# Four moves in the order of work of a one-core decoder layer: compression weights split a turn ahead, a norm behind the values' second blob, late query heads between attention blocks, two output blobs in the projection's buffers

## The chip, the cores and the metric

The kernel runs on one core of a Trainium2 chip. The core has a matrix engine (TensorE, PE in the profile; its weight loads are PEld), a vector engine (VectorE, DVE), a scalar engine (ScalarE, ACT), GpSimd (POOL) and SyncE (SP), whose queue issues most of the loads here. Each engine runs its own instructions in a fixed order and waits on semaphores for the others. The metric is the device time of one execution in microseconds, as the median of several runs; smaller is better. One further execution was taken by the hardware profiler, and every row below is from that one.

## What is computed

The reference is one layer of a hybrid decoder on 512 tokens of width 2048, all in float32:

```python
mod = silu(c) @ w_ada + b_ada            # shift1, scale1, gate1, shift2, scale2, gate2
h   = rms_norm(x, norm1_g) * (1 + scale1) + shift1
u   = h @ w_in      # conv B, C, H | queries | K and V of three branches | gates
y_conv = B * causal_depthwise_conv3(C * H)
k_cmp, v_cmp = compress(K), compress(V)  # gelu(flat @ w1) @ w2 over blocks of 32 tokens
y_attn = compressed, selected and sliding-window attention, summed with sigmoid gates
x   = x + gate1 * ([rms_norm(y_conv) | rms_norm(y_attn)] @ w_out)
h   = rms_norm(x, norm2_g) * (1 + scale2) + shift2
x   = x + gate2 * (relu(h @ w_ff1)**2 @ w_ff2)
out = rms_norm(x, normf_g)
```

There are 8 query heads of 128 in two groups (2 key and value heads), so attention runs as 2 groups times 4 blocks of 128 queries.

## The kernel before

**Splitting.** Every float32 operand of a matmul is split into a high part `hi`, written by ScalarE as float32r, and a low part `lo = x - hi`, written by VectorE. `mm3` (lines 93 to 95) then adds three products: high times high (L93), high times low (L94), low times high (L95). A weight blob of 128 x 1024 thus costs one load of 512 KB (L73 or L781, SyncE's queue), one ScalarE copy (L83 or L789) and one VectorE subtraction (L84 or L790), and feeds 24 matmuls of 512 columns.

**Buffers.** Three pools matter. `mainp` has 29 slots of one tile each for everything that lives long (hidden states `h_m`, `part`, `kwin`, `cs`, conv outputs `y`, queries `q`, the conditioning weights `wa`, and the compression's `chi`, `clo`, `swh`, `swl`). `stage` has three raw buffers `raw`, two `wh` and two `wl`, through which all projection blobs go; a compression blob uses `raw` too but is split into two `mainp` slots (`spare=True`). `ffp` holds the buffers of the later stages (`rw`: six raw ones, `hl`: three split pairs). It is opened when `stage` and the attention's pools are closed and lies where they lay: in the program of before, the three `hl` buffers lie over `attc` and `raw`, the first `rw` buffer over the last `raw` buffer and the first `wh`, the second over both `wh`, the third over the second `wh`, the fourth over the second `wh` and the first `wl`, the fifth over both `wl`, the sixth over the second `wl`. An `ffp` buffer waits for the last reader of each old buffer under it (`reuse_waits="tile"`).

**Order.** Up to line 406 all instructions keep the written order (`pin`). From there on a scheduler orders each engine when the program is built: of the instructions that it estimates to be ready, the one written first goes first. The order on the chip is then fixed; SyncE's queue too is served in order.

**The stages around the change.** (1) The eight conv channels (L510 to 539) call `project` 16 times; each call runs two halves, each with one blob and 24 matmuls. After each half, `tick()` takes one step of the background list, first `compress(0)`, then `compress(1)`, and `more_ada(1)` loads two conditioning blobs and reduces them on VectorE (L134). A compression has two steps that build its operands (`ct`, `chi`, `clo`, L445 to 462), eight steps with one blob each (L464 to 472: load, split, 12 matmuls of 256 columns), and a tail. (2) `row_norm` of the conv output (L543) sums `sacc` over channels with four one-column matmuls (L171), takes a square root on ScalarE (L178, with a table load), a reciprocal, spreads it with a 128 x 512 matmul (L189, L192) and copies it to `rc` (L182), which `mixed` (L581) reads. (3) The values, gates and remaining keys: per group four blobs of 1072 columns, each with 48 matmuls of 268 columns (L548 to 569). (4) The queries; raw heads go to `raws`. `head(n)` (L573) turns one with five VectorE and one ScalarE instruction (`rope_split`). Heads 0 to 3 are made in the background, heads 4 to 7 at L734, ahead of attention. (5) Attention (L743 to 747): per block the scores go through three PSUM buffers `s`; one or two `out_conv` (24 matmuls each, the conv half of the output product) are written behind each block and fill the matrix engine's waits. (6) The attention half's norm, `mixa`, the last two `out_conv` (L753 to 763), then the product with `w_oa` (L812 to 817): eight blobs through `rw` and `hl`, and after each an `ada` with two more `rw` loads. The feed-forward stages follow.

Of the kernel before, what the change touches and what calls it, by code (L numbers as in the profile page):

```python
# [21 lines left out]
NR = 4  # L22
# [18 lines left out]
def hybrid_layer(ctx: ExitStack, tc: tile.TileContext, a, out):  # L41
# [34 lines left out]
    def weights(src, cols=1024, spare=False):  # L76
        raw = load(src, cols)
        if spare:
            wh, wl = slot(F32R, name="swh"), slot(F32R, name="swl")
        else:  # L80
            wh = stage.tile([P, BLOB], F32R, name="wh")
            wl = stage.tile([P, BLOB], F32R, name="wl")
        pin(nc.scalar.activation(wh[:, :cols], raw[:, :cols], AF.Copy))  # L83
        pin(nc.vector.tensor_tensor(out=wl[:, :cols], in0=raw[:, :cols], in1=wh[:, :cols].bitcast(F32),  # L84
                                    op=OP.subtract))
        return wh, wl
# [5 lines left out]
    def mm3(ps, lh, ll, rh, rl, start, stop, more=False):  # L92
        pin(nc.tensor.matmul(ps, lh, rh, start=start, stop=False, skip_group_check=more))  # L93
        pin(nc.tensor.matmul(ps, lh, rl, start=False, stop=False, skip_group_check=more))  # L94
        pin(nc.tensor.matmul(ps, ll, rh, start=False, stop=stop, skip_group_check=more))  # L95
# [72 lines left out]
    def row_norm(bank, square, width, dst, t0=0, t1=NQ):  # L168
        total = bank()
        for t in range(t0, t1):  # L170
            nc.tensor.matmul(total[:, t:t + 1], square[:, t * P:(t + 1) * P], ones[:, 0:1],  # L171
                             start=True, stop=True)
        row_bcast(bank, total[:, t0:t1], width, dst[:, t0 * P:t1 * P])
# [177 lines left out]
    w = (wh0, wl0)  # L351
# [89 lines left out]
    def compress(which, src):  # L441
        pe = cw2[:, which * 32:which * 32 + 32]
        w2 = [cw2[:, 64 + (which * 2 + i) * P:64 + (which * 2 + i + 1) * P] for i in range(2)]
        parts = []
        for hf in range(2):  # L445
            t = slot(name="ct")
            nc.vector.memset(t[:, 1024:SLOT], 0.0)
            tv = t[:, :1024].rearrange("p (l g n) -> p l g n", g=NG, n=32)
            n = 32 - hf
            for g in range(NG):  # L450
                nc.vector.tensor_tensor(
                    out=tv[:, :, g, :n],
                    in0=src[g].rearrange("p (n l) -> p l n", l=16)[:, :, hf:],
                    in1=pe[:, hf * 16:hf * 16 + 16, None].to_broadcast([P, 16, n]), op=OP.add)
            if hf:
                nc.vector.memset(tv[:, :, :, 31:], 0.0)
            hi = slot(F32R, name="chi")
            lo = slot(F32R, name="clo")
            nc.scalar.activation(hi, t, AF.Copy)
            nc.vector.tensor_tensor(out=lo, in0=t, in1=hi.bitcast(F32), op=OP.subtract)  # L460
            parts.append((hi, lo))
            yield
        pc = bank()
        for blk in range(8):  # L464
            wh, wl = weights(a["cmp_w1"][which * 8 + blk], spare=True)
            hi, lo = parts[blk // 4]
            for j in range(4):
                l = blk * 4 + j
                s = slice(j * 256, (j + 1) * 256)
                m = slice((l % 16) * 64, (l % 16) * 64 + 66)  # L470
                mm3(pc[:66, :256], hi[:, m], lo[:, m], wh[:, s], wl[:, s], l == 0, l == 31)
            yield
        hid = temp([P, 256], name="hid")[:64]
        tt = temp([P, 256], name="htt")[:64]
        nc.scalar.activation(hid, pc[:64, :256], AF.Copy)
        nc.vector.tensor_tensor(out=tt, in0=hid, in1=hid, op=OP.mult)
        nc.vector.tensor_scalar(tt, tt, 0.044715, 1.0, op0=OP.mult, op1=OP.add)
        nc.vector.tensor_tensor(out=tt, in0=tt, in1=hid, op=OP.mult)
        nc.scalar.activation(tt, tt, AF.Tanh, scale=math.sqrt(2.0 / math.pi))
        nc.vector.tensor_scalar(tt, tt, 1.0, 0.5, op0=OP.add, op1=OP.mult)  # L480
        nc.vector.tensor_tensor(out=hid, in0=hid, in1=tt, op=OP.mult)
        pt = bank()
        for i in range(2):
            nc.tensor.transpose(pt[:, i * 64:i * 64 + 64], hid[:, i * P:(i + 1) * P], ident[:64, :64])
        hidt = temp([P, 2, NG, 32], name="hidt")
        nc.scalar.activation(hidt.rearrange("p i g n -> p (i g n)"), pt[:, :P], AF.Copy)
        yield
        if which == 0:
            pk = bank()
            for i in range(2):  # L490
                nc.tensor.matmul(pk[:, :64], w2[i], hidt[:, i].rearrange("p g n -> p (g n)"),
                                 start=i == 0, stop=i == 1)
            for g in range(NG):
                split(kslc[g][:, :, :32], pk[:, g * 32:g * 32 + 32])
        else:
            pad = temp([P, 2, NG, P], name="hpad")
            nc.vector.memset(pad, 0.0)
            nc.vector.tensor_copy(pad[:, :, :, :32], hidt)
            for g in range(NG):
                pv = bank()  # L500
                for i in range(2):
                    nc.tensor.matmul(pv[:, :P], pad[:, i, g], w2[i], start=i == 0, stop=i == 1)
                split(vcmp[:, g], pv[:, :P])
# [36 lines left out]
    while background:  # L540
        tick()
    rc = accum("rc")
    row_norm(bank, sacc, 1024, rc)  # L543


    gates = attc.tile([P, NQ, NG, NR, 3], F32, name="gates")
# [1 line left out]
    for g in range(NG):  # L548
        pv = [bank() for _ in range(NQ)]
        for blk in range(4):  # L550
            wh, wl = weights(a["w_v"][g * 4 + blk], BLOB)
            more_ada(1)
            for j in range(4):
                k = blk * 4 + j
                s = slice(j * 268, (j + 1) * 268)
                for t in range(NQ):
                    c = slice(t * P, (t + 1) * P)
                    mm3(pv[t][:, :268], hs[k][:, 0, c], hs[k][:, 1, c], wh[:, s], wl[:, s],
                        k == 0, k == NK - 1)
        for t in range(NQ):  # L560
            if t % 2 == 0:
                vp = pair(F32R, name="vv").rearrange("p h (t c) -> p h t c", t=2)
            vv[g, t] = vp[:, :, t % 2]
            nc.scalar.activation(vv[g, t][:, 0], pv[t][:, :256], AF.Copy)
            nc.vector.tensor_tensor(out=vv[g, t][:, 1], in0=pv[t][:, :256],
                                    in1=vv[g, t][:, 0].bitcast(F32), op=OP.subtract)
            gt = gates[:, t, g].rearrange("p r b -> p (r b)")
            nc.scalar.activation(gt, pv[t][:, 256:268], AF.Tanh, scale=0.5)
            nc.vector.tensor_scalar(gt, gt, 1.0, 0.5, op0=OP.add, op1=OP.mult)
# [3 lines left out]
    def head(n):  # L573
        q = pair(F32R, name="q")
        for _ in rope_split(q, raws[n], SCALE):
            pass
        qs.append(q)
# [153 lines left out]

    for m in range(2):
        out_conv(m)
    for n in range(NR, 2 * NR):  # L734
        head(n)
    ya = []
    m = 2
    for g in range(NG):
        for r in range(NR):
            if r % 2 == 0:  # L740
                y2 = pair(name="ya")
            ya.append(y2[:, r % 2])
        for qb in range(NQ):  # L743
            attention(g, qb)
            for _ in range(1 + g):
                out_conv(m)
                m += 1
# [6 lines left out]
    for j in range(8):  # L754
        y = ya[j]
        nc.vector.scalar_tensor_tensor(out=y, in0=y, scalar=vec[:, V_GA + j:V_GA + j + 1], in1=ra,
                                       op0=OP.mult, op1=OP.mult)
        mt = pair(F32R, name="mixa")
        split(mt, y)
        mixa.append(mt)  # L760
        if j % 4 == 0:
            out_conv(m)
            m += 1
    att.close()
    front.close()

# [17 lines left out]
    def hl_tile():  # L784
        t = ffp.tile([P, 2, 1024], F32R, name="hl", bufs=3)
        return t[:, 0], t[:, 1]

    def hilo(dst, src):
        nc.scalar.activation(dst[0], src, AF.Copy)  # L789
        nc.vector.tensor_tensor(out=dst[1], in0=src, in1=dst[0].bitcast(F32), op=OP.subtract)  # L790
        return dst
# [18 lines left out]
    sacc = accum()  # L810
    pm = [bankf() for _ in range(8)]
    for k in range(8):  # L812
        wh, wl = hilo(hl_tile(), raw_blob(a["w_oa"][k]))
        for i in range(8):
            s = slice(i * P, (i + 1) * P)
            mm3(pm[i], wh[:, s], wl[:, s], mixa[k][:, 0], mixa[k][:, 1], k == 0, k == 7)
        ada(M_G2 * NK + 8 + k, raw_blob)
# [406 lines left out]
```

## Time and profile before

| what | value |
|---|---|
| median of 3 runs | 2229.99 us (2229.52 to 2233.65) |
| the profiled execution, whole | 2229.29 us |
| its span, first to last instruction | 2227.5 us |
| mean granted TensorE clock | 0.979 |
| transferred | 453.62 MB, 204 GB/s mean |

The profile's page gives busy time per engine, a chain of waits, and groups of instructions. Windows are stretches of the span with busy time of each engine (number of instructions in brackets), the clock granted to TensorE (1 is full speed) and DMA. A timeline row gives start and duration in us, engine, line, what is written and read, and in square brackets how long the engine had been idle before it and what ended that. A row of waits gives total us, number of times and the longest.

### The profile page before, as it was taken

To read this page: it belongs to the slowest core of one execution; us is meant where nothing else is said; L and a number is where in the kernel's file an instruction comes from. 1 tells how busy PE (TensorE), PEld (TensorE's weight loads), DVE (VectorE), ACT (ScalarE), POOL (GpSimd) and SP (SyncE) were. 2 spreads that over 40 slices of the span, in tenths; PEclk is the share of its full clock that TensorE was granted. 3 is DMA by queue.
4 is the path that set the end of the run, shared out by engine and by line. 5 is a ranking of instruction groups with operands and counts; after the bars stand their busy time and mean duration, and the time that the engine had idled before them with its cause. 6 is when DMAs were issued, how large, how long until landed. Compare 5 with 4: busy or idle time off the path is not lost.

```text
span 2227.5 us, 37650 instructions
## 1 busy us (share of the span) xinstructions
PE 2134.3 (96%) x14942; PEld 1974.1 (89%) x14942; DVE 1918.9 (86%) x2998; ACT 1009.3 (45%) x1468; POOL 193.6 (9%) x366
## 2 busy tenths in 40 slices
PE   6999899999999989799999999999899999999996
PEld 4777778798787769799999999999899999999996
DVE  8889988777586677999999999999899999999996
ACT  4431333322354434665666556666333333333353
POOL 0000000000000001021111111113211011001000
PEclk8999999999999999899999999999999999999998
DMA  8985677855211165276666666668865466366432
GB/s 343 338 324 179 254 291 284 342 187 192 86 39 57 57 251 189 83 240 200 203 189 197 206 206 201 196 193 277 309 232 210 150 229 237 127 222 244 164 122 95
DMA packets 143984, 453.62 MB, mean 204 GB/s; under 512 B 15808, under 2 KB 20160, under 8 KB 143808
## 3 DMA queue, kind: packets, MB, share of 16 engines
q1 hardware_dynamic: 92192, 323.27, 40.8%
q0 software_dynamic: 51616, 127.95, 17.2%
q8 instruction: 117, 1.92, 0.3%
q14 instruction: 59, 0.48, 0.1%
HBM read 383.00 MB, written 68.16 MB: 203 GB/s over the span
## 4 chain that ended last, share of the span: by engine, by line
PE 77%; DVE 6%; ACT 2%; issue 1%; DMA 1%; POOL 0%; DVEq 0%; ACTq 0%; POOLq 0%
PE pf L95 19%; PE pf L93 19%; PE pf L94 19%; PE ps L95 4%; PE ps L94 4%; PE ps L93 4%; PE pw L95 1%; PE pw L93 1%; PE pw L94 1%; DVE hl L790 1%; PE pt L709 1%; PE pv L93 1%; PE pv L94 1%; ACT hl L789 0%; PE pv L95 0%
## 5 line engine op out<-in xcount | busy, mean ns | idle before, releaser
L95 PE MATMUL pf<-tk,hl 128*128 128x256 f32 x3576 | 1006.0, 282 | 12.7 <-DVE hl L790 12.7
L93 PE MATMUL pf<-tk,hl 128*128 128x256 f32 x3576 | 1008.3, 282 | 9.9 <-ACT hl L789 9.2
L94 PE MATMUL pf<-tk,hl 128*128 128x256 f32 x3576 | 1006.4, 282 | 1.2 <-DVE tk L861 1.2
L95 PEld LDWEIGHTS pf<-tk,hl 128*128 128x128 f32 x3576 | 677.4, 190 | 15.2 <-DVE hl L790 15.2
L93 PEld LDWEIGHTS pf<-tk,hl 128*128 128x128 f32 x3576 | 678.6, 190 | 12.5 <-ACT hl L789 11.8
L94 PEld LDWEIGHTS pf<-tk,hl 128*128 128x128 f32 x3576 | 677.8, 190 | 1.6 <-DVE tk L861 1.5
L789 ACT ACTIVATE hl<-rw 128x1024 fp32r<-128x1024 f32 x266 | 281.0, 1057 | 300.6 <-PE pf L95 267.4
L790 DVE TENSOR_TENSOR hl<-rw,hl 128x1024 fp32r<-128x1024 f32 x266 | 324.0, 1218 | 32.2 <-ACT hl L789 31.7
L789 ACT ACTIVATE hl<-sg 128x1024 fp32r<-128x1024 f32 x189 | 200.3, 1061 | 264.0 <-PE pf L95 243.7
L790 DVE TENSOR_TENSOR hl<-sg,hl 128x1024 fp32r<-128x1024 f32 x189 | 230.3, 1219 | 41.9 <-ACT hl L789 40.9
L134 DVE SCALAR_TENSOR_TENSOR scr<-wa,cs 128x1024 bf16<-128x1024 f32 x176 | 210.1, 1218 | 3.3 <-DMA wa<-in_w_ada 3.2
L83 ACT ACTIVATE wh<-raw 128x1024 fp32r<-128x1024 f32 (+1 forms) x103 | 108.8, 1060 | 219.4 <-PE ps L94 106.2
L84 DVE TENSOR_TENSOR wl<-raw,wh 128x1024 fp32r<-128x1024 f32 (+1 forms) x103 | 126.2, 1226 | 54.1 <-ACT wh L83 53.5
L864 DVE TENSOR_TENSOR sg<-sg,rw 128x1024 f32<-128x1024 f32 x126 | 153.4, 1218 | 0.9
L95 PE MATMUL ps<-h_m,wl 128*128 128x512 f32 x360 | 142.7, 396 | 2.4 <-DVE wl L84 2.4
L93 PE MATMUL ps<-h_m,wh 128*128 128x512 f32 x360 | 142.7, 396 | 1.5 <-DVE part L384 1.0
L94 PE MATMUL ps<-h_m,wh 128*128 128x512 f32 x360 | 141.7, 394 | 0.0
L1038 DVE SCALAR_TENSOR_TENSOR x<-pf,mod,x 128x256 f32<-128x256 f32 x256 | 119.9, 478 | 14.2 <-PE pf L95 11.9
L93 PE MATMUL ps<-h,wh 128*128 128x512 f32 x280 | 113.4, 405 | 7.2 <-ACT wh L83 3.3
L95 PE MATMUL ps<-h,wl 128*128 128x512 f32 x280 | 114.0, 407 | 3.9 <-DVE wl L84 3.9
L94 PE MATMUL ps<-h,wh 128*128 128x512 f32 x280 | 113.2, 404 | 0.0
L1004 POOL DMA_DIRECT2D g<-gt x192 | 101.0, 532 | 86.9 <-DVE gt L861 81.5
(308 smaller groups left out, 2981.6 us busy)
## 6 DMA issues: line engine op xcount, KB each, us to landing
rw<-in_w_f SPq DMA_DIRECT2D x262, 512.0 KB, 4.4
wa<-in_w_ada SPq DMA_DIRECT2D x176, 512.0 KB, 6.0
tk<-g POOLq DMA_DIRECT2D x114, 512.0 KB, 8.6
g<-gt POOLq DMA_DIRECT2D x192, 256.0 KB, 4.9
raw<-in_w_conv SPq DMA_DIRECT2D x32, 512.0 KB, 6.7
g<-gb POOLq DMA_DIRECT2D x36, 256.0 KB, 2.3
raw<-in_w_kv SPq DMA_DIRECT2D x16, 512.0 KB, 5.4
raw<-in_w_cv SPq DMA_DIRECT2D x16, 512.0 KB, 4.1
```

The costliest lines, as they stand in the source:

```text
L83: pin(nc.scalar.activation(wh[:, :cols], raw[:, :cols], AF.Copy))
L84: pin(nc.vector.tensor_tensor(out=wl[:, :cols], in0=raw[:, :cols], in1=wh[:, :cols].bitcast(F32), op=OP.subtract))
L93: pin(nc.tensor.matmul(ps, lh, rh, start=start, stop=False, skip_group_check=more))
L94: pin(nc.tensor.matmul(ps, lh, rl, start=False, stop=False, skip_group_check=more))
L95: pin(nc.tensor.matmul(ps, ll, rh, start=False, stop=stop, skip_group_check=more))
L134: pin(nc.vector.scalar_tensor_tensor(out=scr, in0=w, scalar=1.0, in1=cs[i].rearrange("p a b -> p (a b)"), op0=OP.mult, op1=OP.mult, accum_ ...
L709: nc.tensor.transpose(pt[:, r * P:(r + 1) * P], probs[b, r][:, kb * P:(kb + 1) * P], ident)
L789: nc.scalar.activation(dst[0], src, AF.Copy)
L790: nc.vector.tensor_tensor(out=dst[1], in0=src, in1=dst[0].bitcast(F32), op=OP.subtract)
L864: nc.vector.tensor_tensor(out=dst, in0=x, in1=y, op=op)
L1004: nc.gpsimd.dma_start(out=gd[p // 4][idx[j]][p % 4 // 2][:, p % 2], in_=g[:, j])
L1038: nc.vector.scalar_tensor_tensor(out=xm, in0=src, scalar=gate, in1=xm, op0=OP.mult, op1=OP.add)
```

## The change

`compress` takes the weights of blob 0 at the end of its second operand step and those of each later blob behind the matmuls of the one before, where it took them ahead of its own matmuls. The norm's call moves from in front of the values into their first group, behind the second blob's matmuls. Heads 4 to 7 are no longer made in a row ahead of attention, but one behind each block of the first group, ahead of that block's `out_conv`. The first two `w_oa` blobs are taken by `weights` (buffers `raw`, `wh`, `wl`) at the end of attention, before the pools are closed, and the loop over `w_oa` uses them for k = 0 and 1.

```diff
@@ compress
             parts.append((hi, lo))
+            if hf:
+                w = weights(a["cmp_w1"][which * 8], spare=True)
             yield
         pc = bank()
         for blk in range(8):
-            wh, wl = weights(a["cmp_w1"][which * 8 + blk], spare=True)
+            wh, wl = w
             hi, lo = parts[blk // 4]
...
                 mm3(pc[:66, :256], hi[:, m], lo[:, m], wh[:, s], wl[:, s], l == 0, l == 31)
+            if blk < 7:
+                w = weights(a["cmp_w1"][which * 8 + blk + 1], spare=True)
             yield
@@ conv norm and values
     rc = accum("rc")
-    row_norm(bank, sacc, 1024, rc)
...
                         k == 0, k == NK - 1)
+            if g == 0 and blk == 1:
+                row_norm(bank, sacc, 1024, rc)
@@ attention
         out_conv(m)
-    for n in range(NR, 2 * NR):
-        head(n)
...
             attention(g, qb)
+            if g == 0:
+                head(NR + qb)
             for _ in range(1 + g):
@@ output product
             m += 1
+    oa = [weights(a["w_oa"][k]) for k in range(2)]
     att.close()
     front.close()
...
     for k in range(8):
-        wh, wl = hilo(hl_tile(), raw_blob(a["w_oa"][k]))
+        wh, wl = oa[k] if k < 2 else hilo(hl_tile(), raw_blob(a["w_oa"][k]))
```

## The prediction

> **What bounds the kernel now.** I read the page's busy times first, then who waited for whom on the matrix engine, then windows of 20 us, and last the timelines of the four places that the change touches.
>
> ```profile
> span 2227.5 us, 37650 instructions
> PE 2134.3 (96%) x14942; PEld 1974.1 (89%) x14942; DVE 1918.9 (86%) x2998; ACT 1009.3 (45%) x1468; POOL 193.6 (9%) x366
> ```
>
> The matrix engine is busy 96% of the span; time can be won only where it stands still, or runs at a low clock after standing still. It idles 93 us in all. The windows show how much of that lies where the change works:
>
> ```profile
> 260.00:280.00 20.00, 14.48 (x74) 11.72 (x72) 19.92 (x34) 8.01 (x9) 0.00 (x0) 0.96 0.74 277
> 280.00:300.00 20.00, 17.81 (x75) 14.51 (x76) 16.32 (x26) 7.18 (x8) 0.00 (x0) 0.78 0.76 277
> 340.00:360.00 20.00, 20.00 (x94) 16.48 (x93) 19.13 (x32) 6.39 (x7) 0.00 (x0) 1.00 0.87 322
> 600.00:620.00 20.00, 17.47 (x88) 14.73 (x87) 18.63 (x57) 9.47 (x31) 0.00 (x0) 0.83 0.13 43
> 680.00:700.00 20.00, 18.55 (x88) 14.69 (x88) 11.27 (x37) 8.14 (x27) 0.00 (x0) 0.91 0.02 6
> 780.00:800.00 20.00, 14.83 (x62) 10.86 (x60) 15.94 (x25) 9.57 (x17) 0.00 (x0) 0.93 0.11 39
> ```
>
> Columns: window, length, then busy time (instructions) of PE, PEld, DVE, ACT, POOL, then granted clock, DMA share, GB/s. Lost are 5.5 + 2.2 us around the first compression, 2.5 in the first attention block, 5.2 ahead of `w_oa`, and in each the clock falls under 1. The second compression (340 to 360) loses nothing.
>
> **Part A, the compression.** The waits of 260 to 300, engine by engine:
>
> ```profile
> 274.64 0.34 PE L94 MATMUL ps<-swl,chi 128*66 128x256 f32 x1 [1.67 <-DVE swl L84]
> 280.37 0.48 PE L93 MATMUL ps<-swh,chi 128*66 128x256 f32 x1 [4.22 <-ACT swh L83]
> 282.67 0.80 PE L95 MATMUL ps<-h,wl 128*128 128x512 f32 x1 [1.82 <-DVE wl L84]
> 273.62 0.42 SPq L73 DMA_DIRECT2D raw<-in_cmp_w  x1
> 279.26 1.06 ACT L83 ACTIVATE swh<-raw 128x1024 fp32r<-128x1024 f32 x1 [0.81 <-DMA raw<-in_cmp_w]
> 281.39 1.22 DVE L84 TENSOR_TENSOR wl<-raw,wh 128x1024 fp32r<-128x1024 f32 x1
> ```
>
> Three waits, 7.7 us. The longest is for the third blob's load, issued only at 273.62, when a raw buffer came free. With each split written a turn earlier, its raw buffer is free a turn earlier and that load with it: I take the 4.2 us as gone. The other two are VectorE's, which is busy 19.92 of 20 us. No VectorE work is removed; one split more (1.22 us, the row at 281.39) now stands ahead of each conv blob's subtraction. So A = -4.2 + 1.2 = **-3.0**. The ends: all three waits gone and with them the slow stretch behind (14 matmuls of 512 columns between 282.67 and 288.79, 0.43 us apart where they need 0.23: 2.9 us), -10.6; nothing gained and the split more paid, +1.2. The number of loads and instructions is unchanged; two slots of `mainp` are held a turn longer (a rival below).
>
> **Part B, the conv norm.**
>
> ```profile
> 440.15 0.40 PE L95 MATMUL ps<-h_m,wl 128*128 128x512 f32 x1
> 443.46 1.05 PE L171 MATMUL ps<-ones,sacc 128*128 128x1 f32 x8 [2.91 <-DVE sacc L539]
> 445.90 2.04 PE L192 MATMUL ps<-dg,ones 128*128 128x512 f32 x2 [1.38 <-DVE dg L189]
> 446.95 1.21 PE L93 MATMUL ps<-wh,h 128*128 128x268 f32 x1
> 449.08 0.34 PE L93 MATMUL ps<-wh,h 128*128 128x268 f32 x1
> 449.39 0.28 PE L95 MATMUL ps<-wh,h 128*128 128x268 f32 x1
> 441.53 1.28 DVE L84 TENSOR_TENSOR wl<-raw,wh 128x1072 fp32r<-128x1072 f32 x1 [0.25 <-ACT wh L83]
> 786.42 1.10 PE L192 MATMUL pt<-dg,ones 128*128 128x512 f32 x2
> ```
>
> From the last conv matmul's end (440.15 + 0.23) to the first value matmul pass 6.57 us. The norm's own matmuls need 1.05 + 1.10 = 2.15 of that (the second as it ran at full clock at 786.42). Up to 449.08 the values' first seven matmuls take 2.13 us where at 0.123 us each (449.39 and after) they need 0.86: 1.27 more. The second value blob was split by 442.8, so the first was before; nothing else stops the values from starting at 440.4. B = -(6.57 - 2.15) - 1.27 = **-5.7**. Behind the second blob, at about 440.4 + 2 x 5.9 = 452.2 (48 matmuls of 0.123 each), `sacc` (443.4) is long done. The chain from L171 to L192 waits through a table load, the root, a reciprocal and L189:
>
> ```profile
> 783.75 1.28 ACT L178 ACT_TABLE_LOAD   x1
> 785.05 0.30 ACT L178 ACTIVATE rs<-tot,eps 128x4 f32<-128x4 f32 x1
> 785.38 0.18 DVE L179 RECIPROCAL rs<-rs 128x4 f32<-128x4 f32 x1 [0.38 <-ACT rs L178]
> 785.59 0.69 DVE L189 TENSOR_TENSOR dg<-vec,rs 128x512 f32<-128x512 f32 x1
> ```
>
> 2.5 us, covered by the third blob's matmuls; uncovered, B shrinks to -3.2, its other end. `rc` then comes near 457.6 instead of 448.6; its readers (`mixed`) feed the conv half of the output product, over 100 us later. No load is moved.
>
> **Part C, the late heads.**
>
> ```profile
> L281 DVE SCALAR_TENSOR_TENSOR q<-rs,q x8: 679/688/694, 544.5 to 608.6; 128x512 fp32r<-128x512 f32 x8
> 602.55 0.19 DVE L673 TENSOR_TENSOR pc<-s,cst 128x32 f32<-128x32 f32 x1
> 602.89 0.47 PE L663 MATMUL s<-kslc,q 128*128 128x160 f32 x1 [2.41 <-DVE pc L673]
> ```
>
> A head is five VectorE instructions of about 0.69 us; four heads are 13.7 us (20 x 0.69), and they end at 608.6, inside the first attention block. There a score buffer comes free only with L673, which stands behind them, and the matrix engine waits 2.41 us. Written behind the block, the heads fill VectorE's pauses instead. They don't vanish: each instruction can hold a short reduction of blocks 0 to 3 by up to 0.69 us. The second group's first block (680 to 700) has no heads and still idles 1.45 us at clock 0.91. I take 600 to 620 to become like it: (2.53 - 1.45) + 20 x (0.91 - 0.83) = 1.1 + 1.6 = **-2.7**. Ends: the idle 2.5 and all of the clock's 20 x 0.17 = 3.4 us, -5.9; only moved about, 0.
>
> **Part D, the first two output blobs.**
>
> ```profile
> 795.84 0.74 DVE L640 SCALAR_TENSOR_TENSOR x<-pw,mod,raw 128x512 f32<-128x512 f32 x1
> 796.61 0.33 SPq L781 DMA_DIRECT2D rw<-in_w_oa  x1
> 796.99 0.90 SPq L781 DMA_DIRECT2D rw<-in_w_ada  x2
> 797.93 0.43 SPq L781 DMA_DIRECT2D rw<-in_w_oa  x1
> 798.60 1.38 DVE L90 TENSOR_TENSOR mixa<-ya,mixa 128x512 fp32r<-128x512 f32 x2
> 801.71 0.80 PE L93 MATMUL pf<-mixa,hl 128*128 128x512 f32 x1 [6.55 <-ACT hl L789]
> 804.85 1.06 ACT L789 ACTIVATE hl<-rw 128x1024 fp32r<-128x1024 f32 x1 [3.19 <-DMA rw<-in_w_oa]
> 815.63 0.40 PE L95 MATMUL pf<-mixa,hl 128*128 128x512 f32 x1
> SPq L781 <- DVE x L640: 24.9, 1, 24.9
> ```
>
> Now the first `rw` load waits for the last `out_conv`'s residual, because it lies over a `raw` buffer; the matrix engine stands 6.55 us, and k = 1 ends at 815.9. After: k = 0 has its high part early and starts at 795.5. VectorE is full with `mixa` to 800.0, so the low part ends at 801.2 (1.22 us); 16 high-part matmuls (0.23 each) can go first, to 799.2, then 2.0 us of waiting; 32 matmuls later, at 808.6, k = 1 ends. That is 7.3 us ahead.
>
> What is late next is k = 2. All six `rw` buffers lie over the `wh` and `wl` that k = 0 and 1 now use until then. SyncE's queue has, in written order, two `ada` loads for k = 0, two for k = 1, then k = 2's blob. The first may go when k = 0 is done; the second lies over both `wh` and waits for k = 1's last L94, at 808.3, and three loads wait behind it. In the burst of before, the fourth load, issued as the second `rw<-in_w_oa` row, landed 804.85 - 796.61 = 8.2 us after the first issue. So k = 2's blob lands at 816.5, is copied by 817.6, and k = 2 starts 1.7 us later than now, waits 0.4 more for its low part (1.22 us, of which two slow matmuls of 0.43 cover the most) and, after 9 us of rest, runs 12 matmuls at the slow spacing (12 x 0.20 = 2.4). D = 1.7 + 0.4 + 2.4 = **+4.5**, a loss. Ends: written order kept inside k = 0, so that only two matmuls go ahead of the low part (3.2 more rest, and slow after it, 2.4), +10.1; no blocking at all, -7.3. I take the blocking, since the row of 24.9 us shows that these buffers do wait for what lies under them.
>
> Whether the 2.0 us rest inside k = 0 slows the clock is open: after 1.67 us (274.64) the next matmuls ran at full spacing, after 2.41 (602.89) they didn't. I take the nearer row, no. [...] By the trace's stricter reading the sum would be 2.4 us higher.
>
> **Sum.** -3.0 - 5.7 - 2.7 + 4.5 = -6.9 on the profiled execution's own 2229.3 us (span 2227.5 and 1.8 around it): 2222.4. That execution lies 0.7 under the median of the runs, so the forecast is 2223.
>
> **Rivals.**
>
> *D isn't blocked.* If the loads for k = 2 can start at 796.6 as now, D is -7.3 and the time 2229.3 - 3.0 - 5.7 - 2.7 - 7.3 = 2210.6. For it: the trace shows only the first `rw` load waiting, not the others. Against it: the order of SyncE's queue and the buffers' places.
>
> *VectorE only moves its work.* A = +1.2 and C = 0, with B and D as forecast: 2229.3 + 1.2 - 5.7 + 4.5 = 2229.3, no change. For it: 19.92 of 20 us in 260 to 280.
>
> *Slots run out: slower.* Two split blobs at once hold four of 29 `mainp` slots, so `wa` loads wait for compression matmuls, and the conv blob's load queues behind them:
>
> ```profile
> SPq L147 <- PE ps L95: 10.8, 8, 3.9
>   ACT wh L83: 35.7, 11
> ```
>
> The first row is SyncE's queue waiting for slots that compression matmuls release, 1.35 us each; the second, from who waits for the conv blobs' loads, shows that ScalarE already waits 11 times for one. At one such wait more per blob, all reaching the matrix engine, 16 x 1.35 = 21.6 us come on top in place of A's gain: 2229.3 + 21.6 - 5.7 - 2.7 + 4.5 = 2247.0. It decides from the turn on in which a conv blob is split later than the one before it is used up. Against it: 340 to 360 is full at 20.00 with the same loads, and the scheduler sends a load that is ready ahead of one that waits for a slot.
>
> **Chances.** Forecast 0.50, D unblocked 0.20, work only moved 0.17, slots 0.13. What a measurement of this kernel tells from no change is about 0.2%, 4.5 us (its runs spread over 4.1). Within the forecast, where A and D have wide ends, I give 0.72 to faster, 0.24 to same, 0.04 to slower; moved work is same at 0.75 and slower at 0.2; the outer two count whole. That makes 0.57 faster, 0.25 same, 0.18 slower. The forecast's own ends, taken as not all at once, are 2213 to 2232. The range reaches below to the unblocked case and above past the moved work, but not to the slots: 2207 to 2236.
>
> **What would show it.** A: the matrix engine's 4.2 us wait for `swh` is gone and 300 to 440 stays full. B: values start right behind the last conv matmul, and L192 waits under 0.5 us. C: 600 to 620 reads like 680 to 700. D: `w_oa` starts near 795.5 on the old scale, the second `rw` load comes only when k = 1 is done, and a wait of about 9 us for ScalarE's `hl` stands ahead of k = 2. I am wrong if that wait is missing, or if new waits appear at conv blobs between 300 and 440.

## The result, and the profile after

The changed kernel takes 2225.53 us (median of 10 runs, 2221.58 to 2228.79), the kernel before beside it 2231.85 (10 runs): the ratio is 0.9978, 95% interval 0.9970 to 0.9986, so 3.1 to 6.7 us faster. The forecast was 2223. The total came out; three of its four terms did not.

The page's head and the windows of 20 us of the changed kernel (columns as before):

```profile
span 2222.4 us, 37638 instructions
PE 2133.1 (96%) x14942; PEld 1971.6 (89%) x14942; DVE 1918.5 (86%) x2998; ACT 1008.6 (45%) x1468; POOL 193.6 (9%) x366
```

```profile
260.00:280.00 20.00, 13.85 (x75) 10.97 (x73) 18.41 (x30) 7.43 (x8) 0.00 (x0) 0.92 0.66 235
280.00:300.00 20.00, 17.73 (x72) 14.02 (x73) 17.07 (x26) 8.85 (x9) 0.00 (x0) 0.82 0.78 291
440.00:460.00 20.00, 20.00 (x161) 19.52 (x159) 15.35 (x27) 6.24 (x8) 0.00 (x0) 1.00 0.37 130
580.00:600.00 20.00, 17.62 (x84) 15.21 (x83) 9.85 (x32) 6.72 (x21) 0.00 (x0) 0.86 0.29 105
600.00:620.00 20.00, 19.63 (x103) 15.23 (x102) 15.37 (x40) 9.47 (x28) 0.00 (x0) 0.97 0.00 1
780.00:800.00 20.00, 18.61 (x78) 14.34 (x77) 16.60 (x26) 7.33 (x11) 0.00 (x0) 1.00 0.39 134
800.00:820.00 20.00, 17.05 (x66) 13.07 (x65) 17.54 (x29) 5.12 (x5) 0.00 (x0) 0.91 1.01 399
```

Read them against the old ones. The first compression (260 to 300) is no fuller: 31.58 us busy of 40, before 32.29. The values' window (440 to 460) is full. The first attention block's loss has moved along with the block, which starts 6.2 us earlier and so now lies in 580 to 600 (17.62 at clock 0.86; before 17.47 at 0.83). `w_oa` starts early, at 788.96, and 2.95 us of rest are left in 800 to 820.

Windows shift against each other, so the stages are better compared by the time between two matmuls that both kernels have. All entries are differences of start times in the traces (us):

| stage, from one matmul to the next named | before | changed | A only (e1) | B only (e2) | C only (e3) | D only (e4) | e9 | e10 | e11 |
|---|---|---|---|---|---|---|---|---|---|
| conv and compression: last projection to last conv matmul | 216.24 | 217.17 | 217.94 | 214.62 | 215.02 | 215.03 | 211.19 | 205.08 | 215.31 |
| norm and values: to the last value matmul | 55.43 | 50.22 | 56.44 | 50.19 | 56.43 | 56.32 | 50.19 | 50.23 | 50.19 |
| queries, attention: to the last `out_conv` matmul | 299.19 | 299.10 | 299.84 | 299.43 | 298.86 | 299.85 | 298.97 | 298.60 | 298.82 |
| `w_oa`: to its last matmul | 54.33 | 51.08 | 52.34 | 54.28 | 52.68 | 51.02 | 51.48 | 53.39 | 51.43 |
| to the 201st feed-forward matmul that has `tk` | 94.03 | 97.27 | 95.68 | 94.04 | 95.87 | 96.41 | 95.47 | 97.44 | 96.62 |

(e9 to e11 come below.) The two profiled executions differ by 5.1 us. Of that, 1.7 us was there before the first changed instruction: the last projection matmul starts at 223.92 and at 222.24. The stages between give +0.9, -5.2, -0.1, -3.2 and +3.2, and what follows gives +1.0. The columns also show how far one execution scatters where nothing was changed: the first row reads 214.62 to 216.24 without part A, the fourth 52.34 to 54.33 without part D.

**A: the same six loads, another blob behind them.** SyncE's queue in the kernel before, a row that the prediction does not show, and the next one:

```profile
263.64 9.93 SPq L147 DMA_DIRECT2D wa<-in_w_ada  x6
273.62 0.42 SPq L73 DMA_DIRECT2D raw<-in_cmp_w  x1
269.94 1.22 DVE L84 TENSOR_TENSOR swl<-raw,swh 128x1024 fp32r<-128x1024 f32 x1
```

The third row is VectorE's last read of the raw buffer that this load takes (by the addresses of the built program, the first compression blob's). The buffer was free at 271.16, and the load went 2.5 us later.

The same queue in the changed kernel, and the matrix engine's waits of half a microsecond or more there:

```profile
263.84 9.96 SPq L147 DMA_DIRECT2D wa<-in_w_ada  x6
273.86 0.42 SPq L73 DMA_DIRECT2D raw<-in_w_conv  x1
274.33 0.42 SPq L73 DMA_DIRECT2D raw<-in_cmp_w  x1
```

```profile
268.61 0.33 PE L93 MATMUL ps<-swh,chi 128*66 128x256 f32 x1 [0.54 <-ACT swh L83]
274.76 0.33 PE L94 MATMUL ps<-swl,chi 128*66 128x256 f32 x1 [1.55 <-DVE swl L84]
282.00 0.80 PE L93 MATMUL ps<-h,wh 128*128 128x512 f32 x1 [5.73 <-ACT wh L83]
```

In both kernels six conditioning loads occupy SyncE's queue for ten microseconds, since three of them (four in the changed kernel) wait for `mainp` slots. Before, the third compression blob stood behind them; now that blob is ahead of them and a conv blob stands behind. The 4.2 us wait for `swh` is gone and a 5.7 us wait for `wh` has come.

**B** went as forecast. The values' first matmul follows the last conv matmul directly, at 439.64; the norm's matmuls come 12 us later and wait for nothing:

```profile
439.41 0.39 PE L95 MATMUL ps<-h_m,wl 128*128 128x512 f32 x1
439.64 0.29 PE L93 MATMUL ps<-wh,h 128*128 128x268 f32 x1
451.48 0.95 PE L171 MATMUL ps<-ones,sacc 128*128 128x1 f32 x8
452.84 1.28 ACT L178 ACT_TABLE_LOAD   x1
455.96 1.02 PE L192 MATMUL ps<-dg,ones 128*128 128x512 f32 x2
```

**C.** The first attention block, now without a head in it (VectorE and the matrix engine):

```profile
591.89 1.23 DVE L84 TENSOR_TENSOR wl<-raw,wh 128x1024 fp32r<-128x1024 f32 x1 [0.97 <-ACT wh L83]
593.03 0.48 DVE L672 TENSOR_REDUCE nm<-s 128x1 f32<-128x128 f32 x2
593.84 0.19 DVE L678 TENSOR_TENSOR pc<-s,cst 128x32 f32<-128x32 f32 x1 [0.33 <-ACT p L675]
594.09 0.34 PE L668 MATMUL s<-kslc,q 128*128 128x160 f32 x1 [2.38 <-DVE pc L678]
```

The wait for `pc` is 2.38 us; it was 2.41. VectorE has pauses all round, but in its fixed order the subtraction of an `out_conv` blob stands first and the scores' maximum behind it; VectorE idles 0.97 us for that subtraction's `wh`, while the first scores' four matmuls had started at 589.97 to 590.27. In the kernel before, two instructions of a head stood right ahead of the instruction that ended the wait (602.55):

```profile
601.13 0.69 DVE L269 TENSOR_TENSOR rt<-qr,rot 64x512 f32<-64x512 f32 x1
601.84 0.69 DVE L271 TENSOR_TENSOR rt<-qr,rot 64x512 f32<-64x512 f32 x1
```

So other work stands in the place of the heads, and the wait is as long.

**D.** SyncE's queue and the two subtractions that release it, then `w_oa`'s first matmul, the rest inside k = 0, and the 49th matmul:

```profile
779.33 17.45 SPq L787 DMA_DIRECT2D rw<-in_w_ada  x4
796.83 0.42 SPq L787 DMA_DIRECT2D rw<-in_w_oa  x1
```

```profile
793.65 0.33 SPq L787 DMA_DIRECT2D rw<-in_w_ada  x1
795.98 0.80 SPq L787 DMA_DIRECT2D rw<-in_w_ada  x2
```

```profile
792.36 1.22 DVE L84 TENSOR_TENSOR wl<-raw,wh 128x1024 fp32r<-128x1024 f32 x1
794.70 1.22 DVE L84 TENSOR_TENSOR wl<-raw,wh 128x1024 fp32r<-128x1024 f32 x1
788.96 0.40 PE L93 MATMUL pf<-mixa,wh 128*128 128x512 f32 x1
793.63 0.73 PE L95 MATMUL pf<-mixa,wl 128*128 128x512 f32 x2 [1.32 <-DVE wl L84]
804.23 0.51 PE L93 MATMUL pf<-mixa,hl 128*128 128x512 f32 x1 [2.43 <-ACT hl L795]
```

The first `rw` load goes at 779.33, long before `w_oa`; the second at 793.65 and the third at 795.98 follow the two subtractions' ends (793.58, 795.92), that is, they wait for `raw`, not for `wh` and `wl`. The blob of k = 2 is the fourth load from 793.65 on and the matrix engine waits 2.43 us for it, not 9. The addresses in the built program say why: in the kernel before, the first `ffp` buffer asked for is an `hl` (its place is taken before the blob's), so the three `hl` lie at the pool's start, over `attc` and `raw`. In the changed kernel k = 0 needs no `hl`, the first buffer asked for is the `rw` of the first `ada`, and the two kinds change places: `rw` over `attc` and `raw`, `hl` over the last `raw`, `wh` and `wl`.

### The profile page after: what moved, and what is told of

It is laid out like the page before. It is cut to its first block, busy times and chain, and to the rows that moved or that the text cites. A ratio compares the mean times of both kernels' runs of the same rounds, so it can differ in the third digit from the quotient of the medians.

```text
span 2222.4 us, 37638 instructions
## 1 busy us (share of the span) xinstructions
PE 2133.1 (96%) x14942; PEld 1971.6 (89%) x14942; DVE 1918.5 (86%) x2998; ACT 1008.6 (45%) x1468; POOL 193.6 (9%) x366
## 4 chain that ended last, share of the span: by engine, by line
PE 77%; DVE 13%; ACT 5%; DMA 3%; issue 2%; SPq 0%; POOL 0%; DVEq 0%; ACTq 0%; POOLq 0%
PE pf L95 19%; PE pf L93 19%; PE pf L94 18%; PE ps L95 5%; PE ps L94 5%; PE ps L93 5%; DVE scr L134 3%; DVE wl L84 2%; DVE hl L796 1%; ACT wh L83 1%; PE pw L94 1%; PE pw L95 1%; PE pw L93 1%; PE pt L714 1%; PE pv L93 1%
## 5 line engine op out<-in xcount | busy, mean ns | idle before, releaser
L95 PE MATMUL pf<-tk,hl 128*128 128x256 f32 x3576 | 1006.2, 282 | 11.4 <-DVE hl L796 11.4
L95 PEld LDWEIGHTS pf<-tk,hl 128*128 128x128 f32 x3576 | 677.6, 190 | 14.0 <-DVE hl L796 13.9
L95 PE MATMUL ps<-h_m,wl 128*128 128x512 f32 x360 | 142.8, 397 | 2.4 <-DVE wl L84 2.4
L95 PE MATMUL ps<-h,wl 128*128 128x512 f32 x280 | 113.6, 406 | 2.4 <-DVE wl L84 2.4
```

## Experiments

**Each part alone**, on the kernel before: the diff of the change, cut to one part.

> Part A alone on the kernel before. Theory 1 (the stall near 270 to 284 us comes from SyncE's queue: six conditioning loads that wait for mainp slots stand ahead of one weight blob, and the change only swaps which blob that is): the matrix engine still stands 6 to 8 us there, now for the conv blob's wh, and the time moves by 0 to -1.5 us. Theory 2 (the prediction: the third compression blob's load was late for want of a raw buffer): -3.0 us, the 4.2 us wait gone and nothing in its place.

> Part B alone. Theory 1 (from the changed kernel's trace: the values start 6.6 us earlier, and 1.4 us is given back where the norm's own matmuls now stand): -5.2 us, at 0.2% or a little more. Theory 2 (the prediction): -5.7. Either way nearly the whole 6.3 us between the two kernels is this part; if it gives less than 3 us, other parts carry the gain and both are wrong.

> Part C alone. Theory 1 (the first attention block's stall is not the heads' but that of the score chain behind a weight subtraction on VectorE, so it stays): a wait of 2 to 2.5 us for pc stays in the first block and the time moves by less than 0.7 us either way. Theory 2 (the prediction): -2.7 us, 20 us of the first block at the clock and idle time of the second group's first block.

> Part D alone. Theory 1 (rw lies over attc and raw in this program and hl over the projection's wh and wl, so that k=2's blob is late by some 2.4 us instead of 9): w_oa ends about 3 us sooner, of which a part is lost again to the clock near 900 to 940 us: -0 to -3 us. Theory 2 (the prediction: the six rw buffers lie over wh and wl): +4.5 us, a wait of about 9 us ahead of k=2.

Measured against one median of before, 2230.44 us (28 runs); the last column is the ratio times it:

| kernel | us | ratio, 95% interval | us against before |
|---|---|---|---|
| A, split (e1) | 2232.07 | 1.0006, 0.9998 to 1.0015 | +1.3 (-0.4 to +3.3) |
| B, norm (e2) | 2223.59 | 0.9969, 0.9957 to 0.9981 | -6.9 (-9.6 to -4.2) |
| C, heads (e3) | 2229.58 | 0.9996, 0.9987 to 1.0004 | -0.9 (-2.9 to +0.9) |
| D, blobs (e4) | 2228.18 | 0.9990, 0.9981 to 0.9998 | -2.2 (-4.2 to -0.4) |

Part B carries the change. Part A loses or gives nothing; -3.0 is outside its interval. C is not told from nothing, and -2.7 is just inside its interval. D is a small gain and no loss. The waits named by theory 1 are there, in e1, e3 and e4 (one row of each):

```profile
283.48 0.80 PE L93 MATMUL ps<-h,wh 128*128 128x512 f32 x1 [5.67 <-ACT wh L83]
```

```profile
601.13 0.34 PE L663 MATMUL s<-kslc,q 128*128 128x160 f32 x1 [2.03 <-DVE pc L673]
```

```profile
811.97 0.49 PE L93 MATMUL pf<-mixa,hl 128*128 128x512 f32 x1 [2.47 <-ACT hl L790]
```

**The conditioning loads from another queue** (e5 on the changed kernel, e6 on part B alone):

```diff
-                nc.sync.dma_start(out=w, in_=a["w_ada"][2 * n + i])
+                nc.gpsimd.dma_start(out=w, in_=a["w_ada"][2 * n + i])
```

> The changed kernel with the conditioning loads of L147 issued from GpSimd's queue instead of SyncE's (GpSimd does nothing else in that stage). Theory 1 (the stall of the first compression is a weight blob that stands in SyncE's queue behind conditioning loads waiting for slots): the 5.7 us wait for the conv blob's wh near 282 us is gone, at most 2 us of waits for swl stay, and with the slow matmuls behind it the time falls by 5 to 8 us against the changed kernel, to 2218-2220. Theory 2 (VectorE, busy 9 to 10 of 10 us there, is the limit): VectorE's work is the same, so the waits only change their names and the time moves by less than 1.5 us. Theory 3: loads from GpSimd's queue start later than from SyncE's and VectorE waits for wa; slower.

> Part B alone (the conv norm moved), and the conditioning loads from GpSimd's queue; the compression as before the change. Theory 1 (queue): the 4.2 us wait for swh near 280 us is gone too, without any change to the compression, and the time falls by 5 to 8 us against part B alone (2223.6), to 2216-2219. Theory 2 (the third blob waits for a raw buffer, as the prediction had it): the wait stays at some 4 us, and the time with it.

e5: 2228.39 us, ratio 0.9989 (0.9980 to 0.9999), no faster than the changed kernel; its runs spread from 2221 to 2232. e6: 2227.35, 0.9990 (0.9981 to 0.9998), slower than part B alone. The matrix engine's longest wait in that stretch, in e5 and in e6, and VectorE in e6:

```profile
274.19 0.50 PE L93 MATMUL ps<-h,wh 128*128 128x512 f32 x1 [2.49 <-ACT wh L83]
```

```profile
286.46 0.48 PE L94 MATMUL ps<-swl,chi 128*66 128x256 f32 x1 [7.50 <-DVE swl L84]
```

```profile
280.84 1.23 DVE L134 SCALAR_TENSOR_TENSOR scr<-wa,cs 128x1024 bf16<-128x1024 f32 x1 [2.60 <-DMA wa<-in_w_ada]
```

In e5 the 5.7 us wait is gone, as theory 1 said, a shorter one of 2.5 is left, and the conv stage takes 212.96 us, 4.2 less than in the changed kernel; but the 5 to 8 us that theory 1 expected of the whole did not come. In e6 theory 1 missed altogether: the weight blob is no longer held up in the queue, but VectorE, whose order is fixed too, stands 2.6 us before a reduction whose load comes late (issued on GpSimd's queue at 272.79, landed 8.0 us later, the wait that theory 3 of e5 named), and with the subtractions behind it `swl` comes 7.5 us late. So the conditioning work holds up the weights in two places, in SyncE's queue and on VectorE; freeing one is not enough. Where these two kernels lose time later, and why e5 spreads so much, stays open; the profiled execution of e5 (2221.48 us) is the fastest of its twelve and can't show it.

**The placement in D.** One line more, so that an `hl` is asked for first again (e7); and in e8 the same, with the blobs ahead of the conditioning loads:

```diff
+    hl0 = hl_tile()
     for k in range(8):
-        wh, wl = oa[k] if k < 2 else hilo(hl_tile(), raw_blob(a["w_oa"][k]))
+        wh, wl = oa[k] if k < 2 else hilo(hl0 if k == 2 else hl_tile(), raw_blob(a["w_oa"][k]))
```

```diff
+    hl0 = hl_tile()
+    nxt = raw_blob(a["w_oa"][2])
     for k in range(8):
-        wh, wl = oa[k] if k < 2 else hilo(hl_tile(), raw_blob(a["w_oa"][k]))
+        wh, wl = oa[k] if k < 2 else hilo(hl0 if k == 2 else hl_tile(), nxt)
...
-        ada(M_G2 * NK + 8 + k, raw_blob)
+        if 2 <= k < 7:
+            nxt = raw_blob(a["w_oa"][k + 1])
+        if k:
+            ada(M_G2 * NK + 7 + k, raw_blob)
+    ada(M_G2 * NK + 15, raw_blob)
```

> The changed kernel with one line more: the first hl buffer is taken ahead of the loop over w_oa, so that hl lies over attc and raw again and the six rw over the projection's wh and wl, as the prediction had assumed. Theory 1 (the prediction's blocking was right for that placement, and wrong only because the change itself swaps the two): the second rw load starts when k=1 is done, 8 to 10 us of waiting stand ahead of k=2, w_oa ends 6 to 8 us later than in the changed kernel, and the whole is 4 to 8 us slower than it. Theory 2 (placement isn't what matters): k=2 starts within 1 us of the changed kernel's.

> As e7 in placement, but k=2's blob is loaded first of all rw loads, each next blob ahead of the conditioning loads, and the conditioning work one turn later. Theory 1: its buffer waits for k=0 alone, its blob lands at about 800.5 and k=2 follows k=1 with under 1 us of waiting; w_oa ends 2 to 3 us before the changed kernel's. What of that is left at the end tells whether time won here is kept: if the stage behind it is limited by VectorE and the clock, less than half; if not, all of it (2222.5-2223.5).

e7: 2232.47 us, ratio 1.0011 (1.0002 to 1.0019), 6.9 us above the changed kernel's median. SyncE's queue and the wait ahead of k = 2:

```profile
798.95 7.05 SPq L787 DMA_DIRECT2D rw<-in_w_ada  x4
806.05 0.43 SPq L787 DMA_DIRECT2D rw<-in_w_oa  x1
```

```profile
813.55 0.79 PE L93 MATMUL pf<-mixa,hl 128*128 128x512 f32 x1 [8.85 <-ACT hl L795]
```

This is the wait that the prediction described: about 9 us forecast, 8.85 measured. The stage takes 56.93 us, 2.6 more than before the change and 5.9 more than in the changed kernel. One line that computes nothing decides between a gain and a loss.

e8: 2230.77 us, 1.0003 (0.9994 to 1.0011). k = 2 no longer waits and `w_oa` takes 49.29 us, the shortest of all (1.8 us less than in the changed kernel, where 2 to 3 were expected). But the conditioning loads that were put off now stand ahead of the next stage's blobs, and the matrix engine waits there:

```profile
824.63 6.77 SPq L787 DMA_DIRECT2D rw<-in_w_ada  x6
832.22 16.81 SPq L787 DMA_DIRECT2D rw<-in_w_oa  x7
846.04 0.38 PE L93 MATMUL pf<-mixa,hl 128*128 128x256 f32 x1 [3.06 <-ACT hl L795]
```

More than the gain is given back there: from the last `out_conv` to the 201st feed-forward matmul e8 takes 151.9 us, the changed kernel 148.4.

**The conditioning work held back.** The pairs of the sixth to eighth half of the conv stage are skipped; the list is worked off in order, so that they come at its end:

```diff
             tick()
-            more_ada(1)
+            halves_done[0] += 1
+            if halves_done[0] not in (6, 7, 8):
+                more_ada(1)
```

> The changed kernel, with the conditioning pairs of the sixth to eighth half of the conv stage held back, so that they come behind the last ones (same 176 loads and sums in all). Ahead of the third compression blob then stands no waiting conditioning load in SyncE's queue, and VectorE has 7.3 us less to do in that stretch. Theory 1 (the stall is made by these loads): the 5.7 us wait for wh and the 1.5 us for swl are gone, the clock stays full from 260 to 300 us, and the time falls by 5 to 9 us against the changed kernel, to 2217-2220. Theory 2 (a conv blob or a compression blob is late for another reason, a raw buffer or ScalarE): a wait of 3 us or more stays and the time moves by less than 2 us.

> As e9, but the compression as before the change (parts B, C and D, and the held pairs). It shows what the early split is worth when nothing stands in the queue. Theory 1 (the split a turn ahead wins nothing by itself): within 2 us of e9. Theory 2 (the prediction's part A: a raw buffer comes free a turn earlier): 3 us or more slower than e9, with a wait for swh of some 4 us.

> The changed kernel without part A (B, C and D as they are). From part A alone (+1.4 us, and +1.7 at the end of the conv stage in its trace) theory 1 says 1 to 3 us faster than the changed kernel, 2222.5 to 2224.5. The prediction's part A says 3 us slower than it, 2228.5.

Against a median of before of 2231.38 us (17 runs): e9 2222.94, ratio 0.9959 (0.9945 to 0.9972); e10 2218.94, 0.9944 (0.9932 to 0.9957); e11 2225.28, 0.9975 (0.9964 to 0.9986). The windows of e9, then those of e10:

```profile
260.00:280.00 20.00, 17.13 (x88) 13.59 (x87) 17.96 (x25) 10.38 (x12) 0.00 (x0) 0.97 0.44 146
280.00:300.00 20.00, 20.00 (x95) 16.61 (x94) 16.57 (x23) 5.85 (x7) 0.00 (x0) 0.95 0.82 308
```

```profile
260.00:280.00 20.00, 20.00 (x101) 16.54 (x99) 18.81 (x26) 9.64 (x11) 0.00 (x0) 1.00 0.55 193
280.00:300.00 20.00, 19.85 (x104) 16.45 (x103) 16.51 (x25) 5.53 (x6) 0.00 (x0) 1.00 0.90 339
```

And the load of the third compression blob in e10, with the subtraction ahead of it:

```profile
270.27 1.22 DVE L84 TENSOR_TENSOR swl<-raw,swh 128x1024 fp32r<-128x1024 f32 x1
271.52 0.33 SPq L73 DMA_DIRECT2D raw<-in_cmp_w  x1
```

In e10 the stall is gone altogether: 39.85 us busy of 40 at full clock, without any change to the compression. Against e11, which differs from it in nothing but the three pairs, the conv stage is 10.2 us shorter and the whole 6.3. The load now goes 0.03 us after the last reader of its raw buffer (271.49), 3.6 us sooner after the last projection matmul than in e11 (46.3 against 49.9): with the queue clear, the buffer is what it waits for. The held pairs free the queue and VectorE together; these runs do not say how much is due to each. In e9, with the early split, the 5.7 us wait is gone as well, but four short ones are left (two of them 0.71 and 1.29 us, for `wh` and `swh`):

```profile
276.74 0.50 PE L93 MATMUL ps<-h,wh 128*128 128x512 f32 x1 [0.71 <-ACT wh L83]
278.76 0.48 PE L93 MATMUL ps<-swh,chi 128*66 128x256 f32 x1 [1.29 <-ACT swh L83]
```

So the early split costs 6.1 us of the conv stage and 4.0 of the whole when nothing stands in the queue. Theory 1 had expected under 2 for this pair, and 5 to 9 us for e9 against the changed kernel, of which it brought 2.6 by the medians and 4.2 by the ratios: both too favourable to the split, and the prediction's part A, which had e10 3 us slower than e9, has the wrong sign. e11 is no faster than the changed kernel within the intervals (1 to 3 us were expected); its conv stage is 1.9 us shorter. e10 is the fastest kernel of this study, and its interval lies below the changed kernel's.

**No late heads at all** (the second group's attention takes heads 0 to 3 again, so the output is not the layer's):

```diff
             if g == 0:
-                head(NR + qb)
+                qs.append(qs[qb])
```

> The changed kernel with heads 4 to 7 left out of it: the second group of queries uses heads 0 to 3 again. It bounds what moving the heads could win. Theory 1 (the heads lie in VectorE's pauses wherever they stand, and the first block's stall belongs to the score chain): the wait for pc in the first block stays at 2 to 2.5 us, and the time falls by less than 1.5 us. Theory 2 (the prediction: the heads cost the first block 2.7 us before, and the other blocks a part of it now): 2 to 4 us less.

e12: 2228.52 us, ratio 0.9985 (0.9976 to 0.9993), no faster than the changed kernel. The first block still waits:

```profile
595.68 0.50 PE L668 MATMUL s<-kslc,q 128*128 128x160 f32 x1 [2.22 <-DVE pc L678]
```

Leaving the heads out wins nothing against the kernel that has them behind the blocks, and moving them there, alone, was not told from nothing (e3).

## Why the total was right and its terms were not

| term | forecast | alone, timed | stage in the traces |
|---|---|---|---|
| A, split | -3.0 | +1.3 (-0.4 to +3.3) | +2.8 |
| B, norm | -5.7 | -6.9 (-9.6 to -4.2) | -5.9 |
| C, heads | -2.7 | -0.9 (-2.9 to +0.9) | -0.4 |
| D, blobs | +4.5 | -2.2 (-4.2 to -0.4) | -1.6 at the end of `w_oa`, -0.1 forty us into the feed-forward |
| sum | -6.9 | -8.7 | -3.6 |

The last column compares means over the profiled kernels with and without the part. For A the conv stage reads 217.2 to 219.0 us in five kernels with the split (the changed one, e1, e7, e8, e12) and 214.6 to 216.2 in five without it (before, e2, e3, e4, e11). For B the values read 50.2 in all ten with it and 55.4 to 56.4 in the four without. For C eight kernels mean 298.9, five mean 299.3, and the two groups overlap. For D seven and five kernels are compared (e7 and e8 are left out). The whole change measured -4.9 (-6.7 to -3.1): between the two sums, and each sum is uncertain by more than it differs from that.

**A: wrong, in its cause.** The step that failed is "issued only at 273.62, when a raw buffer came free". The buffer was free 2.5 us before that (271.16); the load went at 273.62 because the conditioning loads ahead of it in the queue went no sooner. Splitting a turn earlier therefore could not remove the wait; the next blob in the queue took it over. The buffer is only the second cause in line: it sets the load's time in e10, where the queue is clear. The rival "VectorE only moves its work" had +1.2 for this part, the right size by another road: e10 shows that the stretch has no stall when VectorE and the queue are rid of three pairs of conditioning work, and e9 that the early split then costs time of its own. The prediction saw the row with 19.92 of 20 us, and a row with SyncE's waits for slots, and used them for rivals but not for the term itself. The rival with slots had the mechanism of the changed kernel's wait, a conv blob late behind `wa` loads that wait for slots; but those loads waited before the change too, and it happens once with 5.7 us and not sixteen times. Of the new waits at conv blobs between 300 and 440 that the prediction named as a sign against itself there is one, of 0.33 us at 384.54, and one of 0.8 to 1.5 us near that place in e1, e7, e8 and e12; the kernels without the split have none over 0.25 us there but one of 0.47 us in e6.

**B: right**, step by step: the values start right behind the conv, the second value blob covers `sacc`, and the third covers the chain through root and reciprocal; L192 waits for nothing where up to 0.5 us were allowed.

**C: wrong, in its cause.** The step that failed is "I take 600 to 620 to become like" the window with the second group's first block. The heads did stand ahead of the instruction that ended the stall, but taking them away did not shorten it: without them in the block (the changed kernel, e3) and without them anywhere (e12) the wait is 2.0 to 2.4 us. By the rows, what is late then is the first maximum, which stands on VectorE behind a weight subtraction (591.89, ending at 593.12); whether another order there would win the 2.2 us was not tried, so this cause is read from the rows and not shown by a run.

**D: wrong, in its premise.** The step that failed is "All six `rw` buffers lie over the `wh` and `wl`". That holds for the program before. The change itself moves them, since the place of a buffer kind follows from the order of first use. e7 puts the premise right again and gets the forecast wait, 8.85 us; its cost beside the kernel before is 2.6 us at the end of `w_oa`, where +4.5 was forecast: k = 2 starts 0.9 us later after the last `out_conv` matmul than in the kernel before (21.95 against 21.08) and not 1.7, and the slow matmuls after the rest were 7 or 8 and not 12 (an estimate from e7's window of 800 to 820: 41 matmuls busy for 11.11 us, 1.56 more than 41 x 0.233, at 0.20 more for each slow one). The second `rw` load of that placement goes at 804.72, behind k = 1's last L95 (ends at 804.69): asked for second is the buffer over the second `wl`, not the one over both `wh` that the prediction took, which comes to one matmul's difference. The prediction named its own test: "I am wrong if that wait is missing". It is missing. For the rest inside k = 0, 1.32 us where 2.0 were forecast, the choice that the clock stays up held (1.00 in 780 to 800).

What the earlier end of `w_oa` is worth later isn't settled. The 3.2 us of the profiled execution were given back in the next 95 us, but that stretch scatters from 94.0 to 96.0 us in kernels without part D too. At the end of `w_oa` the two groups overlap as well (51.0 to 53.4 us with part D, 52.3 to 54.3 without). Timed alone D keeps 0.4 to 4.2 us.

The errors of A and C (5.8 and 2.3 us by the traces, 4.3 and 1.8 timed alone, towards slower) and that of D (4.6 and 6.7, towards faster) cancel in part. That the total came close to the forecast is luck, not knowledge of the terms, and the range, 2207 to 2236, is wide enough to hold the kernel before as well.

## What to carry to other kernels

The waits for a transfer had two causes here, a buffer (in e10 the load went 0.03 us after the last reader of its raw buffer) and a queue (in the kernel before it went 2.5 us after that reader): before pricing the removal of one, look at what the same queue issued in the ten microseconds ahead of it, and at what those loads waited for. Here, moving a load past a blocked one only changed which load stood behind it, while taking low-priority work out of the crowded stretch won what reordering the urgent work could not (the conv stage is 10.2 us shorter in e10 than in e11). And when a change removes the first use of a buffer, look at the addresses of the changed program before reasoning about what overlaps what.

## What the runs showed of the hardware

A rest's length alone did not tell whether the clock falls. After the 2.41 us rest at 602.89 in the kernel before the matmuls of 512 columns ran 0.43 us apart, where they had run 0.23 apart ahead of it, and the granted clock was 0.50 from 603 to 608; after e5's 2.49 us (the row at 274.19) its window kept a granted clock of 1.00:

```profile
260.00:280.00 20.00, 17.30 (x85) 13.64 (x85) 17.17 (x26) 5.84 (x6) 3.18 (x6) 1.00 0.78 264
```

After the 2.43 us ahead of 804.23 in the changed kernel, and 0.52 more ahead of 805.49, they ran 0.43 apart from 806.05 to 809.04, at a granted clock of 0.51 in 806 to 808. What makes the difference between such places, no run here shows.

The same instructions did not take the same time in every execution: the start of the last projection matmul, ahead of every change, lies between 222.2 and 225.3 us in the fourteen profiles. Differences of 3 us between two single executions say nothing until they are taken from a common point behind that.
